# Gated linear attention on one core: TensorE's order written down, with small fp32 products in fewer runs

## The chip, the cores and the metric

One Trainium2 chip, one of its cores. The metric is device time in microseconds, from the first to the last instruction of one execution and what lies around it; lower is better. The kernel before took 1204.29 us (median of 3 runs, 1204.18 to 1205.54).

The engines by the names of the profile: PE is TensorE (matmul; PEld its weight loads), DVE is VectorE, ACT is ScalarE, POOL is GpSimd, SP is SyncE, which issues most DMAs. Each engine works through its own list of instructions in order; semaphores tie the lists together.

## The reference, cut to what matters

The program is two layers of a decoder trunk for 512 tokens of width 1024. Layer 1 has chunked gated linear attention (GLA) as its mixer, with 4 heads, keys of 128 and values of 256 per head. The change lies in this mixer alone.

```python
q, k, v, g_lr, og = _split(h @ w_in, GLA_SPLITS)
log_a = jax.nn.log_sigmoid(g_lr @ w_gate_up + gate_bias) / GLA_GATE_NORMALIZER
...
def step(state, inp):                       # one chunk of tokens
    qi, ki, vi, gi = inp                    # gi: cumulative sum of log_a in the chunk
    g_end = gi[:, :, -1, :]
    o_inter = einsum('bhtd,bhdv->bhtv', qi * exp(gi), state)
    decay = exp(where(causal, gi[t] - gi[s], -inf))
    scores = einsum('bhtd,bhsd,bhtsd->bhts', qi, ki, decay)
    o_intra = einsum('bhts,bhsv->bhtv', scores, vi)
    state = exp(g_end) * state + einsum('bhsd,bhsv->bhdv', ki * exp(g_end - gi), vi)
    return state, o_inter + o_intra
...
o = _rms_norm(o, o_norm) * silu(og)
return o @ w_out
```

## The kernel before

**Two kinds of matmul.** The large products (`mm3`, lines 162 to 164) split both operands into a rounded high part and the rest, and add high x high, high x low and low x high: three matmuls of 512, 368 or 336 columns. They make the queries, keys and output gates (`feature`: 24 matmuls each, into a `ps` bank of PSUM) and the values (`Values.step`: 48 matmuls for half of the depth, into all four `ps` banks). Their weights are loaded by SP, rounded by ScalarE (`wh`, line 142) and subtracted by VectorE (`wl`, line 143), three buffers each.

The small products work on plain fp32 and write `pa` banks of PSUM, of which there are four too. A head needs, in this order:

- `base`: VectorE's cumulative sum `G` of the log decays, and the product for the diagonal; `diag` (line 1762): a product with ones that gives the scores' diagonal
- `decay` and `level` (lines 1797 and 1800): the scores are built by levels of blocks of 64, 32, 16, 8 (`lo`) and 4 (`hi`). VectorE and ScalarE make a tile `F` of keys and queries times decays for each level, TensorE multiplies it with itself in tiles of 128x64, one `pa` bank per level, and VectorE copies what the mask keeps into the scores (lines 1808, 1810)
- `decay_pairs` and `level_pairs` (line 1835): the blocks of 2 and 1 together, also in 128x64 tiles; four masked copies (lines 1841, 1846)
- `decay_off` and `off` (line 1879): three transposes of the decayed keys; ScalarE copies them out (`kt`, line 1881)
- `state` (line 1893): the chunk states, six matmul records into two banks; ScalarE and VectorE carry them on (lines 1901, 1896)
- `read` (lines 1917, 1919): scores x values plus queries x states, into two banks; ScalarE squares (line 1923), a root is taken on GpSimd, VectorE scales (line 1927)
- `turn` (line 1934): eight transposes of the head's output into two banks; ScalarE scales them into `oT` (line 1938)

`log_decays` transposes the low-rank gate (line 1711), multiplies it by the gate's up-projection (line 1722) and takes the log sigmoid. `gate` makes an output gate (silu on ScalarE, line 1677), `gated` multiplies it with a turned output. `load_vectors_ffn(1)` turns two vectors of the next block's convolution (line 222), whose DMAs landed near the start of the program. The tiles `F`, `E`, `Es`, `Ec` and `kt` share one pool of eight buffers (`new`).

**What sets the order.** The stage's calls stand at the end of `mixer1`. No engine's order is written down there: a planner orders each engine by the place in the program and by its own estimate of when operands and buffers are ready. In the profile TensorE's order follows the calls, with some groups held back and single large products put between: `diag(0)` stands ahead of `query(w, 2)`; three large products stand between `level(2, lo)` and `read(0)`, and one inside `read(0)`; four stand between `turn(0)` and `state(1)`, three between `level(3, lo)` and `read(1)`, and two, four and four stand around `level(3, hi)` and `off(3)`. Elsewhere in the program, in other stages, TensorE's order is written by hand with `tc.manual_schedule(engines={ET.PE})`: inside this block the instructions of the named engines keep the order of the calls, and the planner still orders the others.

Of the kernel before, what the change touches and what calls it, by code (L numbers as in the profile page):

```python
# [14 lines left out]
ALU = mybir.AluOpType  # L15
# [7 lines left out]
ND = D // P  # L23
# [4 lines left out]
GH, GDK, GDV, GR = 4, 128, 256, 16  # L28
ET = mybir.EngineType
# [27 lines left out]
class Kernel:  # L57
# [1557 lines left out]
    def mixer1(self):  # L1615
# [4 lines left out]
        with tc.tile_pool(name="m1", bufs=1) as mp:  # L1620
# [5 lines left out]
            class Values:  # L1626
# [5 lines left out]
                        self.weights(w_in[:, k0 : k0 + 4, 1024 + c0 : 1024 + c1], 4, v.n, by="a") for k0 in (0, 4)  # L1632
                    ]

                def step(v, i):
                    c0, n, vn = v.c0, v.n, v.vn
                    if i == 0:
                        v.pss = [self.ps() for _ in range(NT)]
                    for k in range(4 * i, 4 * i + 4):
                        for t in range(NT):  # L1640
                            self.mm3(
                                v.pss[t][:, :n], tok(k, t), v.ws[i](k % 4, 0, n), start=k == 0, stop=k == ND - 1
                            )
                    for t in range(NT if i else 0):
                        rt = r[:, t : t + 1]
                        if n > vn:
                            nc.scalar.activation(glr[:, t, :], v.pss[t][:, vn:n], AF.Copy, scale=rt)
                        nc.scalar.activation(vt[t][:, c0 : c0 + vn], v.pss[t][:, :vn], AF.Copy, scale=rt)
# [3 lines left out]
            def pair_w(c0):  # L1652
                return self.weights(w_in[:, :, c0 : c0 + 256], ND, 256)

            def feature(w, c):
                ps = self.ps()
                for k in range(ND):
                    self.mm3(ps, w(k, c * P, (c + 1) * P), xg[k], start=k == 0, stop=k == ND - 1)
                return ps

            def query(w, h):
                o = qT[h] = self.fp.tile([P, S], F32, tag="a0", name=self.nm("qT"))
                nc.vector.scalar_tensor_tensor(
                    out=o, in0=feature(w, h % 2), scalar=float(GDK**-0.5), in1=R, op0=ALU.mult, op1=ALU.mult
                )

            def key(w, h):
                o = kT[h] = self.fp.tile([P, S], F32, tag="a0", name=self.nm("kT"))
                ps = feature(w, h % 2)
                with tc.high_priority(offset=60):  # L1670
                    nc.vector.tensor_tensor(o, ps, R, ALU.mult)
# [32 lines left out]
                nc.vector.tensor_tensor(ws[64:96], w[64:96], t[64:96].bitcast(F32), ALU.subtract)  # L1704
                return ws

            def log_decays():

                ps = self.pa()
                for t in range(NT):  # L1710
                    nc.tensor.transpose(ps[:GR, t * P : (t + 1) * P], glr[:, t, :], self.ident)
                gT = self.sp.tile([P, S], F32R, tag="R", name="gT")
                nc.vector.tensor_copy(
                    gT[:96].rearrange("p (a b) -> p a b", b=P), self.ones[:96].unsqueeze(1).to_broadcast([96, NT, P])
                )
                nc.scalar.activation(gT[:GR], ps[:GR], AF.Copy)
                nc.scalar.activation(gT[64 : 64 + GR], ps[:GR], AF.Copy)
                nc.vector.tensor_tensor(gT[32 : 32 + GR], ps[:GR], gT[:GR].bitcast(F32), ALU.subtract)
                es, pzs = [], []
                for h in range(GH):  # L1720
                    pz = self.pa()
                    mm(pz, wgs[:96, h * GDK : (h + 1) * GDK], gT[:96], start=True, stop=True)
                    e = new()
                    nc.scalar.activation(e, pz, AF.Abs)
                    pzs.append(pz)
                    es.append(e)
                for e in es:
                    nc.scalar.activation(e, e, AF.Exp, scale=-1.0)
                for e in es:
                    nc.scalar.activation(e, e, AF.Ln, bias=1.0)  # L1730
                for h, (e, pz) in enumerate(zip(es, pzs)):
                    la = mp.tile([P, S], F32, tag=f"lah{h}", name=self.nm("la"))
                    nc.vector.scalar_tensor_tensor(
                        out=la, in0=pz, scalar=0.0, in1=e, op0=ALU.min, op1=ALU.subtract
                    )
                    las.append(la)
# [10 lines left out]
            def base(h):  # L1747

                G = Gs[h] = mp.tile([P, S], F32, tag="G", name=self.nm("G"), bufs=2)
                nc.vector.tensor_tensor_scan(  # L1750
                    G, run.rearrange("p a b -> p (a b)"), las[h], 0.0, op0=ALU.mult, op1=ALU.add
                )
                sc = scores[h] = mp.tile([P, GDV * NT], F32, tag="sc", name=self.nm("sc"), bufs=3)

                pr = Fs[h, "diag"] = new()[:, : S // 2]
                nc.vector.tensor_tensor(pr, ev(kT[h]), ev(qT[h]), ALU.mult)
                nc.gpsimd.memset(sc[:, :S], 0.0)

            def diag(h):
                sc = scores[h]  # L1760
                pd = self.pa()[:, : S // 2]
                mm(pd, self.ones, Fs[h, "diag"], start=True, stop=True)
                nc.vector.tensor_tensor(
                    sc[:, :S].rearrange("p (a n b) -> p a n b", a=NT, b=2)[:, :, :, 0],
                    pd.rearrange("p (a n) -> p a n", a=NT),
                    ev(self.ident).unsqueeze(1).to_broadcast([P, NT, P // 2]), ALU.mult,
                )
# [106 lines left out]
            def off(h):  # L1874

                Es, Ec, tot = Fs[h, "off"]
                pt = self.pa()
                for i in range(NT - 1):
                    nc.tensor.transpose(pt[:, i * P : (i + 1) * P], Es[:, i * P : (i + 1) * P], self.ident)
                kt = new()  # L1880
                nc.scalar.copy(kt[:, : 3 * P], pt[:, : 3 * P])
                Fs[h, "kt"] = kt
# [70 lines left out]
            v.step(1)  # L1953
            R = self.spread()
            w = pair_w(0)
            query(w, 0)
            log_decays()
            query(w, 1)
            w = pair_w(512)
            key(w, 0)  # L1960
            key(w, 1)
            w = pair_w(256)
            base(0)
            diag(0)
            decay(0, lo)
            query(w, 2)
            level(0, lo)
            decay(0, hi)
            decay_off(0)
            decay_pairs(0)  # L1970
            query(w, 3)
            w = pair_w(768)
            level(0, hi)
            off(0)
            base(1)
            decay(1, lo)
            key(w, 2)
            level_pairs(0)
            diag(1)
            key(w, 3)  # L1980
            v = Values(0, 336, 336)
            level(1, lo)
            decay(1, hi)
            decay_off(1)
            decay_pairs(1)
            v.step(0)
            level(1, hi)
            off(1)
            base(2)
            decay(2, lo)  # L1990
            v.step(1)
            v = Values(336, 672, 336)
            level_pairs(1)
            diag(2)
            state(0)
            decay(2, hi)
            decay_off(2)
            v.step(0)
            level(2, lo)
            read(0)  # L2000
            decay_pairs(2)
            level(2, hi)
            off(2)
            base(3)
            decay(3, lo)
            v.step(1)
            w = pair_w(2064)
            level_pairs(2)
            diag(3)
            turn(0)  # L2010
            state(1)
            decay(3, hi)
            decay_off(3)
            gate(w, 0)
            level(3, lo)
            read(1)
            decay_pairs(3)
            state(2)
            gate(w, 1)
            turn(1)  # L2020
            w = pair_w(2064 + 256)
            self.load_vectors_ffn(1)
            level(3, hi)
            off(3)
            read(2)
            level_pairs(3)
            gate(w, 2)
            turn(2)
            state(3)
            gated(0)  # L2030
            gated(1)
            gate(w, 3)
            w = pair_w(2064 + 512)
            read(3)
            gated(2)
            gated(3)
            gate(w, 4)
            turn(3)
            gated(4)
            gate(w, 5)  # L2040
            w = pair_w(2064 + 768)
            gated(5)
            for m in (6, 7):
                gate(w, m)
                gated(m)
        return lambda done, then: self.project(self.rows(a["gla_w_out"][0]), ys, done, then)

    def run(self):
# [34 lines left out]
```

## Time and profile before

| | |
|---|---|
| median of 3 runs | 1204.29 us (1204.18 to 1205.54) |
| the profiled execution | 1203.8 us, span 1202.0 us |
| TensorE busy | 1194.0 us, 99% of the span |
| VectorE busy | 989.3 us, 82% |
| ScalarE busy | 681.1 us, 57% |
| GpSimd busy | 43.7 us, 4% |
| chain that ended last | TensorE 89%, VectorE 6%, ScalarE 2% |
| the stage that the change orders | 602.2 to 739.3 us |

How to read the rows: a row of the timeline has the start in us, the duration, the engine, the line, the operation, what it writes and reads, the shapes, and how many neighbours of the same kind it stands for; idle time of the engine before it and what ended that stands in brackets. `128*64` is the part of TensorE's array that a product uses. Matmuls are pipelined, so a record lasts past the start of the next one; what one costs is the distance from start to start. Full fp32 products of 256 columns appear as two records each. A row of a stretch has, after the stretch and its length, the busy time and number of instructions of PE, PEld, DVE, ACT and POOL, the granted clock, the DMA share and GB/s. A row of waits has who waited, for whom, the total, how often and the longest.

### The profile page before, as it was taken

Reading aid. Unit: us, or ns where it says so; the run is one execution under the profiler, and the core shown is the slowest. Engines: PE = TensorE matmul, PEld = TensorE weight load, DVE = VectorE, ACT = ScalarE, POOL = GpSimd, SP = SyncE. Lnnn points to the kernel's source line nnn. Section 1 sums busy time; section 2 is a strip of 40 time slices with the busy share of each in tenths; the row PEclk is TensorE's granted clock in tenths of the full one; section 3 lists DMA queues with packets and bytes.
Section 4 is the critical chain, followed back from the end, with each engine's and each line's share of the span. In section 5 each row is a group of like instructions: output and inputs, shape, how many; then the busy total and the mean of one; then the engine's idle time right before and its main releaser. Section 6 shows DMA issues by size and latency. Waiting matters only on the chain.

```text
span 1202.0 us, 17888 instructions
## 1 busy us (share of the span) xinstructions
PE 1194.0 (99%) x7085; PEld 1037.6 (86%) x7085; DVE 989.3 (82%) x1563; ACT 681.1 (57%) x1109; POOL 43.7 (4%) x64
## 2 busy tenths in 40 slices
PE   9999999999999999999999999999999999999998
PEld 8877788999899889888988988889999999888887
DVE  6786587899999996789769876677999999978595
ACT  7466465656555744566563555565555656645374
POOL 2600000000000000000100000000000000000000
PEclk9999999999999999999999999999999999999999
DMA  7221322323233342232422222313242423322501
GB/s 222 90 88 39 97 79 70 129 83 119 92 104 107 107 139 97 97 106 63 140 66 69 71 71 70 106 54 122 71 140 71 139 72 128 127 88 97 210 1 70
DMA packets 110839, 117.61 MB, mean 98 GB/s; under 512 B 2808, under 2 KB 105778, under 8 KB 110756
## 3 DMA queue, kind: packets, MB, share of 16 engines
q1 hardware_dynamic: 109920, 115.88, 29.7%
q8 instruction: 55, 0.90, 0.3%
q0 software_dynamic: 560, 0.42, 0.3%
q10 hardware_dynamic: 276, 0.18, 0.1%
q14 instruction: 28, 0.23, 0.1%
HBM read 114.37 MB, written 2.10 MB: 97 GB/s over the span
## 4 chain that ended last, share of the span: by engine, by line
PE 89%; DVE 6%; ACT 2%; issue 1%; POOL 1%; DMA 0%; SPq 0%; DVEq 0%; ACTq 0%; POOLq 0%
PE ps L162 11%; PE ps L163 11%; PE ps L164 11%; PE pa L163 7%; PE pa L162 7%; PE pa L164 7%; PE ps L879 6%; PE ps L881 6%; PE ps L880 6%; PE pa L879 2%; PE pa L881 2%; PE pa L880 2%; DVE wl L143 1%; PE ps L1484 1%; PE ps L1483 1%
## 5 line engine op out<-in xcount | busy, mean ns | idle before, releaser
L142 ACT ACTIVATE wh<-raw 128x1024 fp32r<-128x1024 f32 (+4 forms) x146 | 145.8, 999 | 124.5 <-PE ps L163 78.8
L143 DVE TENSOR_TENSOR wl<-raw,wh 128x1024 fp32r<-128x1024 f32 (+4 forms) x146 | 168.1, 1151 | 40.7 <-ACT wh L142 39.9
L826 ACT ACTIVATE wh<-raw 128x1024 fp32r<-128x1024 f32 x84 | 89.2, 1062 | 120.6 <-DVE raw L851 65.1
L939 DVE SCALAR_TENSOR_TENSOR zt<-z,vfa,zt 128x510 f32<-128x510 f32 (+1 forms) x176 | 130.6, 744 | 5.3 <-ACT zt L937 4.7
L827 DVE TENSOR_TENSOR wl<-raw,wh 128x1024 fp32r<-128x1024 f32 x84 | 102.6, 1221 | 21.3 <-ACT wh L826 21.2
L937 ACT ACTIVATE zt<-z,vfb 128x512 f32<-128x512 f32 x88 | 71.0, 810 | 21.5 <-DVE four L990 8.3
L162 PE MATMUL ps<-b,wh 128*128 128x512 f32 x192 | 76.8, 400 | 0.0
L163 PE MATMUL ps<-b,wh 128*128 128x512 f32 x192 | 75.1, 391 | 0.0
L164 PE MATMUL ps<-b,wl 128*128 128x512 f32 x192 | 75.0, 391 | 0.0
L879 PE MATMUL ps<-four,wh 128*128 128x256 f32 x248 | 69.4, 280 | 0.7 <-ACT ps L904 0.7
L163 PE MATMUL pa<-a,wh 128*128 128x512 f32 x176 | 69.0, 392 | 0.0
L163 PE MATMUL pa<-b,wh 128*128 128x512 f32 x176 | 69.0, 392 | 0.0
L162 PE MATMUL pa<-a,wh 128*128 128x512 f32 x176 | 69.0, 392 | 0.0
L162 PE MATMUL pa<-b,wh 128*128 128x512 f32 x176 | 69.0, 392 | 0.0
L881 PE MATMUL ps<-four,wl 128*128 128x256 f32 x248 | 68.8, 277 | 0.0
L880 PE MATMUL ps<-four,wh 128*128 128x256 f32 x248 | 68.6, 277 | 0.0
L164 PE MATMUL pa<-a,wl 128*128 128x512 f32 x176 | 68.4, 389 | 0.0
L164 PE MATMUL pa<-b,wl 128*128 128x512 f32 x176 | 68.4, 389 | 0.0
L162 PE MATMUL ps<-a,wh 128*128 128x512 f32 x128 | 50.6, 395 | 0.0
L162 PE MATMUL ps<-uh,wh 128*128 128x512 f32 x128 | 50.3, 393 | 0.0
L163 PE MATMUL ps<-a,wh 128*128 128x512 f32 x128 | 50.2, 392 | 0.0
L163 PE MATMUL ps<-ul,wh 128*128 128x512 f32 x128 | 50.1, 391 | 0.0
(488 smaller groups left out, 3577.4 us busy)
## 6 DMA issues: line engine op xcount, KB each, us to landing
raw<-in_ffn_w_up_dram SPq DMA_DIRECT2D x44, 1024.0 KB, 5.0
raw<-in_ffn_w_down_dram SPq DMA_DIRECT2D x13, 1024.0 KB, 4.8
raw<-in_hy_w_in_dram SPq DMA_DIRECT2D x8, 1024.0 KB, 5.1
raw<-in_gla_w_in_dram SPq DMA_DIRECT2D x8, 1024.0 KB, 5.2
raw<-in_ffn_w_down_dram SPq DMA_DIRECT2D x8, 768.0 KB, 4.2
raw<-in_ple_w_gate_dram SPq DMA_DIRECT2D x6, 1024.0 KB, 4.8
raw<-in_hy_w_out_dram SPq DMA_DIRECT2D x16, 256.0 KB, 4.0
raw<-in_gla_w_out_dram SPq DMA_DIRECT2D x4, 1024.0 KB, 4.8
```

The lines of the kernel that those rows point to most:

```text
L142: nc.scalar.activation(hv, v, AF.Copy)
L143: nc.vector.tensor_tensor(lv, v, hv.bitcast(F32), ALU.subtract)
L162: mm(out, lh, rh, start=start, stop=False, **kw)
L163: mm(out, lh, rl, start=False, stop=False, **kw)
L164: mm(out, ll, rh, start=False, stop=stop, **kw)
L826: nc.scalar.activation(h, src, AF.Copy)
L827: nc.vector.tensor_tensor(l, src, h.bitcast(F32), ALU.subtract)
L879: mm(out, wh, xh, start=first and j == 0, stop=False, **kw)
L880: mm(out, wh, xl, start=False, stop=False, **kw)
L881: mm(out, wl, xh, start=False, stop=j == ND // 2 - 1, **kw)
L937: nc.scalar.activation(y, z, AF.Identity, scale=w2[:, f : f + 1], bias=bb[:, f : f + 1])
L939: nc.vector.scalar_tensor_tensor(out=y[:, tap:], in0=z[:, : S - tap], scalar=w[:, f : f + 1], in1=y[:, tap:], op0=ALU.mult, op1=ALU.add,)
```

## The change

The calls from `query(w, 0)` to the last `gated(m)` stand inside `tc.manual_schedule(engines={ET.PE})`, so TensorE follows them as written. The calls are reordered: `diag(0)` goes behind `query(w, 2)`, next to `level(0, lo)`; `base` and `decay(h, lo)` of the next head go ahead of `level(h, hi)`, `off(h)`, `level_pairs(h)` and the next `diag`, which stand together; `read(0)`, `level(2, hi)` and `off(2)` stand between the halves of a `v.step(1)`; `load_vectors_ffn(1)` stands ahead of `turn(1)`, and `level_pairs(3)` ahead of `read(2)`. `log_decays` is divided: the transposes and the rounding of the gate (`turned_gates`) come behind `query(w, 0)`, the products in the middle of `query(w, 1)`. For this `feature`, `query` and `step` take a function `mid` that they call halfway.

```diff
-                def step(v, i):
+                def step(v, i, mid=None):
...
                     for k in range(4 * i, 4 * i + 4):
+                        if mid and k % 4 == 2:
+                            mid()
...
-            def feature(w, c):
+            def feature(w, c, mid=None):
                 ps = self.ps()
                 for k in range(ND):
+                    if mid and k == ND // 2:
+                        mid()
...
-            def log_decays():
+            def turned_gates():
...
+                return gT
+
+            def log_decays(gT):
...
+            with tc.manual_schedule(engines={ET.PE}):
+                query(w, 0)
+                gT = turned_gates()
+                query(w, 1, lambda: log_decays(gT))
+                w = pair_w(512)
+                key(w, 0)
+                key(w, 1)
+                w = pair_w(256)
+                base(0)
+                decay(0, lo)
+                query(w, 2)
+                diag(0)
+                level(0, lo)
+                decay(0, hi)
+                decay_off(0)
+                decay_pairs(0)
+                query(w, 3)
+                w = pair_w(768)
+                base(1)
+                decay(1, lo)
+                key(w, 2)
+                level(0, hi)
+                off(0)
+                level_pairs(0)
+                diag(1)
+                key(w, 3)
+                v = Values(0, 336, 336)
+                level(1, lo)
+                decay(1, hi)
+                decay_off(1)
+                decay_pairs(1)
+                v.step(0)
+                base(2)
+                decay(2, lo)
+                v.step(1)
+                v = Values(336, 672, 336)
+                level(1, hi)
+                off(1)
+                level_pairs(1)
+                diag(2)
+                state(0)
+                decay(2, hi)
+                decay_off(2)
+                v.step(0)
+                level(2, lo)
+                decay_pairs(2)
+                base(3)
+                decay(3, lo)
+
+                def reading():
+                    read(0)
+                    level(2, hi)
+                    off(2)
+
+                v.step(1, reading)
+                w = pair_w(2064)
+                level_pairs(2)
+                diag(3)
+                turn(0)
+                state(1)
+                decay(3, hi)
+                decay_off(3)
+                gate(w, 0)
+                level(3, lo)
+                read(1)
+                decay_pairs(3)
+                state(2)
+                gate(w, 1)
+                w = pair_w(2064 + 256)
+                self.load_vectors_ffn(1)
+                turn(1)
+                level(3, hi)
+                off(3)
+                level_pairs(3)
+                read(2)
+                gate(w, 2)
+                turn(2)
+                state(3)
...
+                read(3)
...
+                turn(3)
```

The rest of the calls, shown as `...` at the end, keep their order.

More of the change, by code (lines that the diff above doesn't have):

```diff
@@ L1653, in pair_w, with query @@
                 return self.weights(w_in[:, :, c0 : c0 + 256], ND, 256)
-            def feature(w, c):
+            def feature(w, c, mid=None):
                 ps = self.ps()
                 for k in range(ND):
+                    if mid and k == ND // 2:
+                        mid()
                     self.mm3(ps, w(k, c * P, (c + 1) * P), xg[k], start=k == 0, stop=k == ND - 1)
                 return ps
-            def query(w, h):
+            def query(w, h, mid=None):
                 o = qT[h] = self.fp.tile([P, S], F32, tag="a0", name=self.nm("qT"))
                 nc.vector.scalar_tensor_tensor(
-                    out=o, in0=feature(w, h % 2), scalar=float(GDK**-0.5), in1=R, op0=ALU.mult, op1=ALU.mult
+                    out=o, in0=feature(w, h % 2, mid), scalar=float(GDK**-0.5), in1=R, op0=ALU.mult, op1=ALU.mult
                 )
@@ L1955, in mixer1 @@
             w = pair_w(0)
[L1956 to L2045, printed above, removed]
+            with tc.manual_schedule(engines={ET.PE}):
[74 more added lines that the diff above has]
+                state(3)
+                gated(0)
+                gated(1)
+                gate(w, 3)
+                w = pair_w(2064 + 512)
+                read(3)
+                gated(2)
+                gated(3)
+                gate(w, 4)
+                turn(3)
+                gated(4)
+                gate(w, 5)
+                w = pair_w(2064 + 768)
+                gated(5)
+                for m in (6, 7):
+                    gate(w, m)
+                    gated(m)
```

## The prediction

> **What bounds the kernel now.** I read the page first (busy time, the slices, the chain that ended last), then the busy time of each engine by stretches of the GLA stage, then TensorE's timeline there, and beside each suspicious place VectorE's or ScalarE's timeline. The profiled execution took 1203.8 us, 1202.0 of span and 1.8 around it; the median of the runs is 1204.29, so 0.5 above it.
>
> ```profile
> span 1202.0 us, 17888 instructions
> PE 1194.0 (99%) x7085; PEld 1037.6 (86%) x7085; DVE 989.3 (82%) x1563; ACT 681.1 (57%) x1109; POOL 43.7 (4%) x64
> ```
>
> TensorE is busy 99%: no stage can gain by overlap, only by cheaper transitions or by the few waits that are left. The stage that the change orders runs from the four gate transposes, just behind query 0, to the last turn:
>
> ```profile
> 602.19 0.60 PE L1711 MATMUL pa<-cf,glr 128*16 128x128 f32 x4
> 738.29 1.04 PE L1934 MATMUL pa<-cf,sc 128*128 128x128 f32 x8
> 626.00:646.00 20.00, 20.00 (x163) 16.22 (x162) 19.73 (x51) 8.54 (x17) 0.00 (x0) 1.00 0.12 35
> ```
>
> In the last row, of the stretch 626 to 646, the first engine is TensorE, the third VectorE: busy 20.00 and 19.73 of 20 us, at a granted clock of 1.00. VectorE is as full as TensorE. What TensorE reaches earlier there, it waits for.
>
> **The change, part by part.** Between the two rows above, TensorE now leaves its large products 23 times for small fp32 ones (counted in its timeline). Written down, it leaves them 14 times. What is one such visit worth? Two kinds:
>
> ```profile
> 675.32 0.31 PE L163 MATMUL ps<-wl,b 128*128 128x336 f32 x1
> 675.47 0.32 PE L164 MATMUL ps<-wh,b 128*128 128x336 f32 x1
> 675.72 0.62 PE L1800 MATMUL pa<-F 128*64 128x64 f32 x7
> 676.20 1.57 PE L1797 MATMUL pa<-F 128*64 128x32 f32 x47
> 677.70 0.42 PE L162 MATMUL ps<-wh,b 128*128 128x336 f32 x1
> 677.96 0.32 PE L163 MATMUL ps<-wl,b 128*128 128x336 f32 x1
> ```
>
> Starts count, since matmuls overlap. A product of 336 columns follows the one before after 0.15 us (675.32 to 675.47). The last one before the narrow `128*64` products takes 0.25, the first one behind them 0.26: 0.21 lost at these edges, and about 0.3 with the slower first and last narrow product inside the merged rows. The other kind is full width, `128*128`:
>
> ```profile
> 713.60 0.39 PE L164 MATMUL ps<-b,wl 128*128 128x512 f32 x1
> 713.84 0.49 PE L1879 MATMUL pa<-cf,F 128*128 128x128 f32 x3
> 714.08 0.48 PE L162 MATMUL ps<-b,wh 128*128 128x512 f32 x1
> 714.39 0.40 PE L163 MATMUL ps<-b,wh 128*128 128x512 f32 x1
> ```
>
> From 713.60 to 714.39 are 0.79 us, for two large products (0.23 each) and three transposes (0.11 each): 0.01 over. So leaving the large products for full-width fp32 ones is nearly free; what costs is the change to 64 columns and back. Each head has three such groups (the low levels, the high level, the pairs): twelve before. In the written order every joined pair of them still has `off`'s transposes between, full width, so it is twelve after. Term 1: nine visits fewer at 0.01, **-0.1 us**; bounds 0 and -0.9 (three heads have their high level and pairs joined, 0.3 each, if a return across transposes were free).
>
> The Trainium skill (TensorEngine Tiling, Tiling Modes, Key Properties) says that a change of the tiling mode drains TensorE, while another tile of the same mode does not. That speaks against the change: the joins that save a visit don't save a change of mode. By the opposite reading, that any exchange of large for small products drains, nine visits at 0.3 would give -2.7 instead of -0.1; the trace, with 0.01 and 0.3, goes by the rule.
>
> Term 2, waits that go. The diagonal of head 0 stood alone and too early, and the gate products followed 11 large ones where 12 stand now:
>
> ```profile
> 604.91 0.39 PE L163 MATMUL ps<-b,wh 128*128 128x512 f32 x1
> 605.24 1.20 PE L1722 MATMUL pa<-gT,wgs 96*128 96x512 f32 x4
> 619.89 0.39 PE L164 MATMUL ps<-b,wl 128*128 128x512 f32 x1
> 620.31 0.70 PE L1762 MATMUL pa<-F,ones_r 128*128 128x256 f32 x2
> ```
>
> The product before takes 0.33 and 0.42 in place of 0.23, and the first one behind a wait is slower (the four gate products hold TensorE for 1.04, their 1.20 less the 0.16 by which the last overlaps the next, in place of 0.92): 0.1 more each. That is 0.2 and 0.3, together 0.5 us. But the order also puts `level(0, hi)` and `off(0)` (634.06 to 634.95, 0.89 us) behind `key(w, 2)`, so key 2 is reached 0.89 + 0.5 earlier, at 633.6, and its weights are not there:
>
> ```profile
> 634.06 0.66 PE L1797 MATMUL pa<-F 128*64 128x32 f32 x16
> 634.95 0.47 PE L162 MATMUL ps<-b,wh 128*128 128x512 f32 x1
> 632.87 1.22 DVE L143 TENSOR_TENSOR wl<-raw,wh 128x1024 fp32r<-128x1024 f32 x1
> ```
>
> The low half of key 2's weights is ready at 634.1 by VectorE, which has a full queue from the decay chains and does the same work before it in either order. TensorE waits there for 0.5 us and the gain is gone: **0 us**; bounds -0.5 (VectorE cuts the weights sooner) and +0.2. The second wait in this stretch, for key 3's bank, stays as it is, because `v.step(0)` still follows `level(1, lo)`:
>
> ```profile
> 650.64 0.32 PE L164 MATMUL ps<-wh,b 128*128 128x336 f32 x1
> 651.18 0.43 PE L162 MATMUL ps<-wh,b 128*128 128x336 f32 x1 [0.23 <-DVE kT L1671]
> ```
>
> That is 0.54 for 0.15: 0.4 us that VectorE's order may remove or double; **0**, bounds -0.5 and +0.8.
>
> Term 3, waits that come. All small products write the four `pa` banks. Where a run needs more than four, its later products wait until VectorE or ScalarE has emptied the first. The planner put single large products into these places; the written order takes them out. Four places:
>
> (a) Head 1's high level, transposes, pairs, head 2's diagonal and `state(0)` need six banks. How long are the groups between, and how soon does VectorE empty a high level's bank?
>
> ```profile
> 689.36 0.69 PE L1835 MATMUL pa<-qT,kT 128*64 128x64 f32 x16
> 689.98 0.70 PE L1762 MATMUL pa<-F,ones_r 128*128 128x256 f32 x2
> 636.53 0.59 DVE L1808 COPY_PREDICATED sc<-msk,pa 64x128 f32<-64x128 uint8 x2
> 712.92 0.61 DVE L1808 COPY_PREDICATED sc<-msk,pa 64x128 f32<-64x128 uint8 x2
> ```
>
> Pairs take 0.62, the diagonal some 0.5 (its 0.70 less the overlap), transposes 0.24 to 0.3: `state(0)` comes about 1.5 us behind the high level. The bank was empty at 637.1 for products that ended at 634.7 (2.4 us), and at 713.5 for products that ended at 712.9 (0.6; this group's row is under d). The wait is 0.9 or none: **+0.4 us**, bounds 0 and +0.9.
>
> (b) Pairs of head 2, diagonal 3, `turn(0)`, `state(1)`: six banks again. Before, four large products stood ahead of `state(1)`, and it still started only as ScalarE had emptied `turn(0)`'s bank:
>
> ```profile
> 692.37 1.80 PE L1893 MATMUL pa<-vt,F 128*128 128x256 f32 x6
> 690.69 1.05 ACT L142 ACTIVATE wh<-raw 128x1024 fp32r<-128x1024 f32 x1
> 691.63 0.68 ACT L1938 ACTIVATE oT<-pa,vec 128x512 f32<-128x512 f32 x1
> ```
>
> 692.3 is ScalarE's time, behind a weight cut of 1.05 us that it took first. The four large products (0.23 each) move behind and leave a hole of **+0.9 us**; bounds +0.1 (the turn goes ahead of the cut) and +1.8 (the second half waits as long).
>
> (c) `read(1)` directly behind `level(3, lo)`, which holds all four banks; three large products stood between:
>
> ```profile
> 700.63 0.50 PE L162 MATMUL ps<-b,wh 128*128 128x512 f32 x1
> 701.43 0.60 PE L1917 MATMUL pa<-vt,sc 128*128 128x256 f32 x2
> 700.47 0.41 DVE L1810 COPY sc<-pa 64x256 f32<-64x256 f32 x1
> ```
>
> The first bank is free at 700.9, TensorE would come at 700.6: 0.3 and a slower first product, **+0.4 us**; bounds 0 and +0.8 (the whole gap).
>
> (d) The longest run: two vector transposes, `turn(1)`, high level, transposes and pairs of head 3, `read(2)`: nine banks from four. Ten large products (2 + 4 + 4) filled it:
>
> ```profile
> 711.54 0.48 PE L162 MATMUL ps<-b,wh 128*128 128x512 f32 x1
> 712.21 0.66 PE L1797 MATMUL pa<-F 128*64 128x32 f32 x16
> 715.10 1.02 PE L1917 MATMUL pa<-vt,sc 128*128 128x256 f32 x4
> 711.50 0.66 ACT L1938 ACTIVATE oT<-pa,vec 128x512 f32<-128x512 f32 x1
> 714.01 0.67 ACT L1938 ACTIVATE oT<-pa,vec 128x512 f32<-128x512 f32 x1
> ```
>
> The high level started at 712.21, as ScalarE had finished the first `oT` (711.50 + 0.66), and the second `oT` came only behind a silu, at 714.7. With ScalarE's work in that order, all ten (2.3 us) turn into holes. But the vector transposes now come first and have small copies, and pairs ahead of `read(2)` give ScalarE 0.6 more, so a good part may be covered: **+1.1 us**, about the middle; bounds +0.2 and +2.3. The vector transposes' own DMAs landed long before and add no wait; nothing moves on the queues of SP and POOL, whose issues keep their places around it.
>
> `read(0)` moves from 3 large products behind `level(2, lo)` to 24, so 3.2 us later (21 at 0.15); `turn(0)` still follows it by the high level, 24 large products, pairs and a diagonal, some 5 us, which its squares, root and scalings have: **0**, bounds 0 and +0.5.
>
> Sum: -0.1 + 0 + 0 + 0.4 + 0.9 + 0.4 + 1.1 = +2.7, which makes 1206.5 for an execution like the profiled one and **1206.9** against the median. Behind the stage nothing is edited.
>
> **The rivals.** First, covered: the planner knows the written order and gives its evictions other places, so (a) and (c) cost nothing and (b) and (d) their low ends, 0.1 + 0.2, less 0.1: 1204.5. For it: ScalarE is busy 57% only. Against it: the bank times above are ScalarE's and VectorE's, at two places, (b) and (d), within 0.1 us of TensorE's start.
>
> Second, not slower: the joins pay after all. The array's return across a few transposes costs nothing (three joins, 0.9), and no wait comes while all old ones go (0.5 in term 2, 0.4 for key 3, 0.4 in the late `state(1)`): 1204.3 - 2.2 = 1202.1. It decides if `off`'s transposes inside a run begin and end without the 0.1 us edges. Against it: full width and 64 columns meet there exactly as at the edges that the rows show.
>
> Third, the `F` buffers. Eight exist; `base(2)` and `decay(2, lo)` now stand ahead of `level(1, hi)` and `off(1)`, and ten would be live (`Ec` and `kt` of head 0, three of head 1, one diagonal, four levels). Such a wait exists already:
>
> ```profile
> DVE F L1859 <- PE pa L1800: 1.7, 1, 1.7
> ```
>
> If two levels of head 2, and so for head 3, start that much later each costs 1.2 on top, the 1.7 of this row less about 0.5 that (a) counts already: 1206.9 + 2.4 = 1209.3. Against it: VectorE idled 1.7 us in that very wait.
>
> **How the numbers follow.** Chances: the forecast 0.50, covered 0.33, joins pay 0.07, buffers 0.10. About 0.2% (2.4 us) is what a measurement of this kernel can tell from no change; 1206.7 is that line, so of the forecast's 0.50 0.38 lie above it and 0.12 below. Slower: 0.38 + 0.10 = 0.48, and 0.02 of covered: 0.50. Faster by over 0.2% needs 1201.9: 0.04 of the joins and 0.02 of covered, 0.06. The rest is 0.44. Range: the low ends of (a) to (d) with a gain of 1 us give 1203.6, the rival of the buffers 1209.3 and a little: 1203.4 to 1209.5. The likeliest one's own range is 1205.5 to 1208.5.
>
> **What would show it.** TensorE's timeline of the changed kernel would show 14 visits; edges of 0.1 us still at twelve narrow groups; `state(1)` directly behind `turn(0)` with a hole of 0.5 to 1 us that ends with `oT`; holes ahead of the high level or the pairs of head 3 that end with ScalarE; key 2 waiting for `wl`. The prediction is wrong if the runs pass without holes, or if idle time appears where VectorE's decay factors are waited for.

## The result, and the profile after

The changed kernel took 1210.95 us (median of 6 runs, 1209.86 to 1212.02) against 1204.52 of the kernel before beside it (6 runs, 1203.98 to 1205.74): a ratio of 1.0053, 95% interval 1.0043 to 1.0063. It is 6.4 us slower; the prediction's sum was 2.7, and its range ended at 1209.5.

The profiled execution took 1211.58 us, 7.78 more than the one of before. First its page (the span; TensorE's busy time):

```profile
span 1209.8 us, 17890 instructions
PE 1196.2 (99%) x7085; PEld 1039.7 (86%) x7085; DVE 990.4 (82%) x1563; ACT 682.5 (56%) x1109; POOL 43.6 (4%) x64
```

TensorE still shows 99%: the tenths of a page hide 6 us in 1200. Its timeline at the two ends of the stage shows where they lie:

```profile
602.59 0.60 PE L1715 MATMUL pa<-cf,glr 128*16 128x128 f32 x4
...
746.05 1.03 PE L1942 MATMUL pa<-cf,sc 128*128 128x128 f32 x8
```

From the gate transposes to the last turn are 143.46 us, where they were 136.10: 7.36 of the 7.78 lie in the stage. (Another 0.4 lie in query 0 ahead of it, behind a late copy; the kernel with ten buffers, below, has them too.) The same timeline in the joined runs:

```profile
626.77 1.10 PE L1805 MATMUL pa<-F 128*64 128x32 f32 x31
629.07 0.62 PE L1805 MATMUL pa<-F 128*64 128x32 f32 x15 [1.20 <-DVE sc L1771]
...
667.16 0.70 PE L1770 MATMUL pa<-F,ones_r 128*128 128x256 f32 x2
668.43 1.13 PE L1901 MATMUL pa<-vt,F 128*128 128x256 f32 x4 [0.57 <-ACT F L1889]
670.41 0.70 PE L1901 MATMUL pa<-vt,F 128*128 128x256 f32 x2 [0.85 <-DVE sc L1816]
...
691.81 0.32 PE L164 MATMUL ps<-wh,b 128*128 128x336 f32 x1
693.89 0.69 PE L1843 MATMUL pa<-qT,kT 128*64 128x64 f32 x16 [1.76 <-DVE sc L1935]
695.25 0.90 PE L1770 MATMUL pa<-F,ones_r 128*128 128x256 f32 x2 [0.67 <-DVE sc L1935]
695.94 1.92 PE L1942 MATMUL pa<-cf,sc 128*128 128x128 f32 x8
697.78 2.16 PE L1901 MATMUL pa<-vt,F 128*128 128x256 f32 x6
699.59 0.58 PE L162 MATMUL ps<-b,wh 128*128 128x512 f32 x1
...
718.50 0.66 PE L1805 MATMUL pa<-F 128*64 128x32 f32 x16
720.26 0.52 PE L1887 MATMUL pa<-cf,F 128*128 128x128 f32 x3 [1.10 <-DVE sc L1816]
```

Four places have idle time. Below, a hole is the distance from start to start less what the same step takes where it doesn't wait, here or in a kernel below (691.81 to 693.89 is 2.08, and ahead of narrow products the last large one takes 0.25: 1.83).

| place | hole, us | what ended it |
|---|---|---|
| head 0's low levels | 1.39 | the diagonal's bank, VectorE (L1771) |
| both halves of `state(0)` | 0.67 + 1.14 = 1.81 | ScalarE's copy `kt` (L1889), then the high level's bank |
| ahead of `level_pairs(2)` and of `diag(3)` | 1.83 + 0.74 = 2.57 | `read(0)`'s scalings, VectorE (L1935) |
| head 3's high level to `off(3)` | 1.17 | the high level's bank, VectorE (L1816) |

The eight transposes of `turn(0)` then last 1.92 where the eight of the last turn last 1.03, without a wait. The granted clock explains it. In this profile it changes only at multiples of 3.41 us, counted from where its record begins (6.12 us into the span). By stretches of that length, the column behind POOL's is the clock:

```profile
692.20:695.61 3.41, 1.05 (x18) 0.87 (x18) 2.68 (x8) 1.93 (x4) 0.63 (x1) 1.00 0.00 0
695.61:699.03 3.42, 3.42 (x13) 2.65 (x12) 2.69 (x6) 1.85 (x3) 0.52 (x1) 0.50 0.00 0
699.03:702.44 3.41, 3.41 (x16) 2.85 (x16) 2.20 (x7) 1.00 (x2) 0.00 (x0) 1.00 0.02 5
```

Behind the holes TensorE ran at half its clock for one such stretch. From `diag(3)` to the end of `state(1)` (695.25 to 699.59) are 4.34 us; the same products at full clock take 2.63 (a kernel below: 3.13 with a wait of 0.50 in it), so this costs some 1.7.

Together the holes are 6.94, with the clock 8.6. Against it waits of before are gone: key 3's bank 0.4, the diagonal's 0.3, the gate products' 0.2, and smaller ones.

### The profile page after: what moved, and what is told of

It reads as the page before. It is cut to its first block, busy times and chain, and to the rows that moved or that the text cites. A ratio compares the mean times of both kernels' runs of the same rounds, so it can differ in the third digit from the quotient of the medians.

```text
span 1209.8 us, 17890 instructions
## 1 busy us (share of the span) xinstructions
PE 1196.2 (99%) x7085; PEld 1039.7 (86%) x7085; DVE 990.4 (82%) x1563; ACT 682.5 (56%) x1109; POOL 43.6 (4%) x64
## 4 chain that ended last, share of the span: by engine, by line
PE 89%; DVE 6%; ACT 3%; issue 1%; POOL 1%; DMA 1%; DVEq 0%; ACTq 0%; POOLq 0%
PE ps L162 12%; PE ps L163 12%; PE ps L164 12%; PE pa L163 7%; PE pa L162 7%; PE pa L164 7%; PE ps L879 6%; PE ps L881 6%; PE ps L880 6%; PE pa L879 2%; PE pa L881 2%; PE pa L880 2%; DVE wl L143 1%; PE ps L1484 1%; PE ps L1482 1%
## 5 line engine op out<-in xcount | busy, mean ns | idle before, releaser
L143 DVE TENSOR_TENSOR wl<-raw,wh 128x1024 fp32r<-128x1024 f32 (+4 forms) x146 | 168.1, 1152 | 39.4 <-ACT wh L142 38.3
L164 PE MATMUL ps<-b,wl 128*128 128x512 f32 x192 | 74.8, 390 | 0.0
L164 PE MATMUL pa<-b,wl 128*128 128x512 f32 x176 | 68.4, 389 | 0.0
L164 PE MATMUL pa<-a,wl 128*128 128x512 f32 x176 | 68.4, 389 | 0.0
```

The costliest lines, as they stand in the source:

```text
L143: nc.vector.tensor_tensor(lv, v, hv.bitcast(F32), ALU.subtract)
L164: mm(out, ll, rh, start=False, stop=stop, **kw)
```

## The experiments

Theory A, from the trace after: the written order as such loses what the planner's single large products did for the bank waits. Rival B: a second cause lies in the moved calls, `base` and `decay` of the next head ahead of the high level, which fill the eight `F` buffers. Rival C: the diagonal moved to the low levels. Two more questions are whether a joined run saves anything once no hole is in it, and what the clock costs.

**The calls of before, unmoved, written down**

```diff
+            with tc.manual_schedule(engines={ET.PE}):
-            query(w, 0)
-            log_decays()
+                query(w, 0)
+                log_decays()
...
```

> The calls of the kernel before, unchanged, inside the block that writes TensorE's order down: no call is moved, only the planner's single large products between the groups go (3 and 1 at read 0, 4 ahead of state 1, 3 ahead of read 1, 2, 4 and 4 in head 3's run, 11 in front of the gate products). Theory A (the holes come from writing the order down, since nothing fills the waits for the four pa banks): +2 to +4 us against the kernel before, holes ahead of state 1, read 1, the high level and the transposes of head 3. Theory B (the moved calls are the cause: the joined runs and the later read 0): within 1 us of the kernel before.

Measured: 1211.55 us (1209.8 to 1213.12), ratio 1.006 [1.0045, 1.0075]. That is 7.2 slower without one call moved. Its timeline and its stretches:

```profile
602.47 0.60 PE L1711 MATMUL pa<-cf,glr 128*16 128x128 f32 x4
605.51 1.60 PE L1722 MATMUL pa<-gT,wgs 96*128 96x512 f32 x4 [2.44 <-DVE gT L1718]
606.90 0.63 PE L162 MATMUL ps<-b,wh 128*128 128x512 f32 x1
607.33 0.63 PE L163 MATMUL ps<-b,wh 128*128 128x512 f32 x1
```

```profile
602.68:606.09 3.41, 0.97 (x7) 0.58 (x5) 2.58 (x3) 1.92 (x4) 0.00 (x0) 1.00 0.06 7
606.09:609.50 3.41, 3.41 (x10) 2.67 (x9) 0.00 (x0) 3.38 (x6) 0.00 (x0) 0.50 0.91 299
```

With nothing between the gate's transposes and its products, TensorE waits 2.44 us for VectorE's copies, and in the stretch at half clock behind it large products take 0.43 (606.90 to 607.33) instead of 0.23. The other holes are 1.4 ahead of `state(1)`, 0.6 ahead of head 3's high level, 0.9 behind it and 0.7 ahead of `read(2)`: the places (b) and (d) of the prediction.

**The moved calls, with TensorE's order left to the planner**

```diff
-            with tc.manual_schedule(engines={ET.PE}):
-                query(w, 0)
+            query(w, 0)
...
```

> The moved calls of the changed kernel, but the planner orders TensorE again: by its list it puts 13 large products inside state 0, 5 into pairs, diagonal and turn, 6 behind the high level of head 3, 4 ahead of read 1. Theory A (missing fillers): most of the 6.4 us comes back, about 1206 to 1207; the hole in the low levels of head 0 stays (1.4 us), since the order there is the same. Theory B (the moved calls themselves): the time stays within 1.5 us of the changed kernel, 1209.5 or more.

Measured: 1205.27 us (1204.59 to 1205.69), ratio 1.0008 [0.9999, 1.0018]. The planner put single large products back into most of the runs, and 5.7 of the 6.4 us are gone (5.5 when each kernel is taken against the runs of before beside it). What it left:

```profile
628.08 0.66 PE L1805 MATMUL pa<-F 128*64 128x32 f32 x16 [1.20 <-DVE sc L1771]
...
691.07 0.69 PE L1843 MATMUL pa<-qT,kT 128*64 128x64 f32 x16 [0.54 <-DVE sc L1935]
```

So filled runs hide the cause B too; this run alone doesn't say how much of the loss is B's.

**The diagonal of head 0 ahead of query 2 again**

```diff
+                diag(0)
                 query(w, 2)
-                diag(0)
                 level(0, lo)
```

> The changed kernel with one move undone: the diagonal of head 0 stands ahead of query 2 again, so the run of diagonal and low levels needs four banks instead of five. If the fifth bank is what the last low level waits for, its hole of 1.4 us goes, the old wait of the diagonal (0.3) comes back, and the time falls by about 1 us. Rival: VectorE bounds this stretch; the hole then moves to key 2, which waits for its weights, and the time stays.

Measured: 1209.92 us (1209.73 to 1211.7), ratio 1.0052 [1.0035, 1.0069]. The hole of 1.39 is gone; the diagonal's old wait (0.39) and a wait of key 2 for its weights (0.36) come instead. By this trace 0.6 us is C's; the medians are 1.0 apart, but the runs of the two kernels overlap. The other holes stand unchanged, yet in this execution the clock stayed (its stretches of 3.41 us lie elsewhere here):

```profile
693.29 0.69 PE L1843 MATMUL pa<-qT,kT 128*64 128x64 f32 x16 [1.76 <-DVE sc L1935]
694.65 0.70 PE L1770 MATMUL pa<-F,ones_r 128*128 128x256 f32 x2 [0.67 <-DVE sc L1935]
```

```profile
689.55:692.97 3.42, 1.98 (x13) 1.70 (x12) 2.59 (x9) 3.02 (x7) 1.01 (x1) 1.00 0.51 180
692.97:696.38 3.41, 2.28 (x26) 1.79 (x26) 3.35 (x9) 1.56 (x3) 0.00 (x0) 1.00 0.00 0
```

**Ten `F` buffers instead of eight** in the changed kernel

```diff
-            new = lambda: mp.tile([P, S], F32, tag="F", name=self.nm("F"), bufs=8)
+            new = lambda: mp.tile([P, S], F32, tag="F", name=self.nm("F"), bufs=10)
...
-                ws, t = (mp.tile([P, S], F32R, tag="F", name=self.nm("wgs"), bufs=8) for _ in range(2))
+                ws, t = (mp.tile([P, S], F32R, tag="F", name=self.nm("wgs"), bufs=10) for _ in range(2))
```

> The changed kernel with ten F buffers for eight, nothing else. If the kt copy of off(1) and off(2) starts late because its buffer is taken by the decay factors that are now made earlier, the copy comes right behind the transposes: the first hole of state 0 (0.7 us) goes and the second hole of the run of head 2's pairs (0.9 us) shrinks, together -1 to -2 us. If the buffers don't matter, the time stays within 0.5 us and the holes stay where they are.

Measured: 1206.19 us (1205.62 to 1206.63), ratio 1.0015 [1.0006, 1.0024]: 4.8 less (4.5 when each is taken against the runs of before beside it), and TensorE's order is the same instruction for instruction; VectorE's, which the planner makes, is not. Its timeline:

```profile
667.37 0.70 PE L1770 MATMUL pa<-F,ones_r 128*128 128x256 f32 x2
667.97 1.53 PE L1901 MATMUL pa<-vt,F 128*128 128x256 f32 x6
...
691.06 0.70 PE L1770 MATMUL pa<-F,ones_r 128*128 128x256 f32 x2
691.60 1.04 PE L1942 MATMUL pa<-cf,sc 128*128 128x128 f32 x8
692.98 1.56 PE L1901 MATMUL pa<-vt,F 128*128 128x256 f32 x6 [0.34 <-ACT oT L1946]
694.19 0.59 PE L162 MATMUL ps<-b,wh 128*128 128x512 f32 x1
```

The holes in `state(0)` and at the pairs are gone, and with them the half clock; (b), `state(1)` behind `turn(0)`, shows for the first time (0.50). The low levels (1.37) and `off(3)` (1.17) stay. How the buffers did it shows in the changed kernel's waits (who waits for whom: total, times, longest) and timelines of ScalarE and VectorE:

```profile
DVE F L1867 <- PE pa L1808: 2.6, 1, 2.6
ACT F L1889 <- PE pa L1770: 2.3, 2, 2.0
...
DVE F L1784 <- PE pa L1805: 1.8, 1, 1.8
```

```profile
667.90 0.48 ACT L1889 COPY F<-pa 128x384 f32<-128x384 f32 x1 [0.23 <-PE pa L1770]
```

```profile
687.77 0.42 DVE L1784 TENSOR_TENSOR F<-G 128x256 f32<-128x256 f32 x1
...
691.25 0.41 DVE L1786 TENSOR_TENSOR F<-G 128x256 f32<-128x256 f32 x1
691.59 0.16 DVE L171 TENSOR_SCALAR rs<-ss 128x4 f32<-128x4 f32 x1
...
692.86 0.88 DVE L1935 TENSOR_SCALAR sc<-pa,rq 128x256 f32<-128x256 f32 x2 [0.80 <-POOL rq L172]
```

`kt` needs a tile of the pool and gets one only as `diag(2)`, the product just ahead of `state(0)`, has read its own: the run waits for itself. VectorE's decays wait for tiles in the same way and come late; those of head 3 stand as a block of 3.8 us (687.77 to 691.59) ahead of the root's input for `read(0)` (L171). In the kernel with ten tiles that instruction runs at 687.20.

**Eight buffers, but `base` and the low decays of heads 2 and 3 behind `off` again**; TensorE's order is unchanged

```diff
                 v.step(0)
-                base(2)
-                decay(2, lo)
                 v.step(1)
...
                 off(1)
+                base(2)
+                decay(2, lo)
...
-                base(3)
-                decay(3, lo)
...
                     off(2)
+                    base(3)
+                    decay(3, lo)
```

> The changed kernel with eight F buffers and exactly its TensorE order; only the calls that make heads 2 and 3's running sums and low decay factors (base and decay) stand behind off(1) and off(2) again, as before, so that VectorE's and ScalarE's order changes and the factors no longer take the buffers ahead of the kt copies. If the early factors in eight buffers are the cause, the holes in state 0 (0.7 and 1.0 us) and ahead of head 2's pairs (1.9 and 0.9) go without any more buffers: 1206 to 1207. If the holes come from too few PSUM banks in the joined runs or from read 0's late place, they stay, since TensorE's order is the same: 1209.5 or more.

Measured: 1207.72 us (1206.66 to 1208.04), ratio 1.0026 [1.0016, 1.0037], 3.2 less than the change. Most of the wait in `state(0)` (0.2 is left ahead of the diagonal there) and the holes at the pairs go again, by a second way. In their place `state(1)` waits for the turn, its whole price now bare (a hole of 1.99):

```profile
691.33 1.04 PE L1942 MATMUL pa<-cf,sc 128*128 128x128 f32 x8
694.19 1.56 PE L1901 MATMUL pa<-vt,F 128*128 128x256 f32 x6 [1.82 <-ACT oT L1946]
```

**Ten buffers in the kernel before**

> The kernel before with ten F buffers and nothing else: the control for the run with ten buffers. If the buffers were short only in the new order, it stays within 1 us of the kernel before (1204.3). If ten buffers simply make this stage faster, it falls by as much as the changed kernel did with them, 4 to 5 us.

The edit is that of the run above. Measured: 1203.92 us (1203.49 to 1204.5), ratio 0.9997 [0.9988, 1.0006]. The old calls don't lack tiles; the moved ones do.

**All holes filled**: ten buffers, the diagonal in the middle of query 2, three large products ahead of `state(1)`, six between head 3's high level and `off(3)`, `read(2)` ahead of the pairs

```diff
-                query(w, 2)
-                diag(0)
+                query(w, 2, {4: lambda: diag(0)})
...
-                state(1)
-                decay(3, hi)
-                decay_off(3)
-                gate(w, 0)
+                gate(w, 0, {1: lambda: (state(1), decay(3, hi), decay_off(3))})
...
-                off(3)
-                level_pairs(3)
-                read(2)
-                gate(w, 2)
+                gate(w, 2, {2: lambda: (off(3), read(2), level_pairs(3))})
```

> The changed kernel with ten F buffers and three of its joins opened again by hand: head 0's diagonal in the middle of query 2, three large products between turn 0 and state 1, six between head 3's high level and its transposes, with read 2 ahead of the pairs. With ten buffers holes of 1.4, 0.5 and 1.3 us are left at just these places. If they are waits for banks, all three go, with 0.3 given back at key 2's weights: about 1203.3, 1 us below the kernel before. If VectorE or ScalarE bound these places, the holes move behind the fillers and the time stays above 1205.

Measured: 1204.03 us (1203.32 to 1205.46), ratio 0.9997 [0.9988, 1.0006]. A written order without those holes is as fast as the planner's, with fewer visits, and no faster: the joins save nothing that can be measured. One wait is left, the one that the prediction put at key 2:

```profile
633.89 0.39 PE L163 MATMUL ps<-b,wh 128*128 128x512 f32 x1
634.98 0.50 PE L164 MATMUL ps<-b,wl 128*128 128x512 f32 x1 [0.70 <-DVE wl L143]
```

**Ten buffers, moved calls, planner's order**

> The moved calls with ten F buffers, TensorE's order left to the planner, which now lists one filler of 2 products ahead of state 1 and one of 6 behind head 3's high level. The hole in head 0's low levels (1.4) stays, the one ahead of head 2's pairs (0.7 with eight buffers) goes: about 1204.5. If it is slower than the handwritten order with ten buffers (1206.2), the planner's own VectorE order is at fault.

This combines two edits shown above. Measured: 1204.44 us (1203.48 to 1205.26), ratio 1.0001 [0.9992, 1.0009]. The diagonal's hole of 1.40 stands in it, and the whole is still level with before.

**The calls of before written down, with the gate products in the middle of query 1**

```diff
                 query(w, 0)
-                log_decays()
-                query(w, 1)
+                gT = turned_gates()
+                query(w, 1, lambda: log_decays(gT))
```

> The order before written down call by call took 1211.55 us, with one hole of 2.61 us ahead of the gate products (VectorE empties the transposes' banks behind a feature that was issued earlier) and TensorE's clock at a half for some 4 us behind it. Here the transposes stand ahead of query 1 and the products in its middle, as in the changed kernel; nothing else of that order is moved. If the hole and the low clock behind it (six to nine large products 0.2 us slower each, 1.2 to 1.8 us) both go: 1207 to 1207.8. If the low clock has another cause and stays: about 1209. If the hole only moves to the next wait: 1211 to 1212.

Measured: 1207.93 us (1207.03 to 1209.38), ratio 1.0032 [1.0022, 1.0041]: 3.6 less than without the split. Of ten executions five took 1207.0 to 1207.6 and four 1209.2 to 1209.4. In the profiled one, of 1207.31 us, the hole of 2.6 is gone:

```profile
605.72 1.07 PE L1727 MATMUL pa<-gT,wgs 96*128 96x512 f32 x4
```

1209.8, the fastest execution without the split and the only one of its four with a clock of 1.000, less 2.6 is 1207.2. In the profiled execution without the split, of 1210.96 us, the half clock cost some 1.5 more (six large products at 0.43, the gate products at 1.39 in place of 1.04); the two slower ones weren't profiled.

**The filled kernel, with head 0's high level and `off` ahead of key 2**

```diff
+                level(0, hi)
+                off(0)
                 key(w, 2)
-                level(0, hi)
-                off(0)
                 level_pairs(0)
```

> As the kernel with ten F buffers and large products in three of the small runs (1204.03 us), with the high level and the transposes of head 0 ahead of key 2 again, where the kernel before has them. There TensorE waited 0.86 us for key 2's low weights. If that wait is what is left of the stage's loss, 0.9 us go and the hole at key 2 is under 0.1: 1203.1. If VectorE sets the pace there, the wait comes back a little later (key 3, or the values' first step) and the time stays at 1204.0. One more visit to the large products is 0.01 by the trace and can't be seen; if a visit cost 0.3, it would be 1203.4.

Measured: 1204.15 us (1203.57 to 1204.81), ratio 0.9998 [0.999, 1.0007]. Key 2's wait is gone, and about as much, 1.0, comes back 30 us later, in front of `state(0)`:

```profile
665.45 0.70 PE L1770 MATMUL pa<-F,ones_r 128*128 128x256 f32 x2
667.07 1.53 PE L1901 MATMUL pa<-vt,F 128*128 128x256 f32 x6 [0.92 <-DVE sc L1816]
```

VectorE is as full as TensorE between the two places (busy 30.55 of the 31.00 us from 636 to 667), which fits that it sets the pace there: the place where TensorE waits could be chosen here, the wait not. No order tried beats the kernel before by more than a measurement can tell.

## Why the prediction was wrong

**Term 1 was right.** TensorE leaves its large products 14 times, and the visit that joins head 0's high level, transposes, pairs and head 1's diagonal keeps the edges of its parts:

```profile
640.76 0.66 PE L1805 MATMUL pa<-F 128*64 128x32 f32 x16
641.35 0.55 PE L1887 MATMUL pa<-cf,F 128*128 128x128 f32 x3
641.83 0.69 PE L1843 MATMUL pa<-qT,kT 128*64 128x64 f32 x16
642.44 0.70 PE L1770 MATMUL pa<-F,ones_r 128*128 128x256 f32 x2
642.79 0.58 PE L162 MATMUL ps<-b,wh 128*128 128x512 f32 x1
```

Over what its products take without edges this visit has 0.63 us; its two halves had 0.28 and 0.35 as visits of their own. The rival of paying joins falls.

**Term 2 saw the gain and not the price.** It counted the diagonal's move to the low levels as a wait that goes. But a diagonal and four low levels need five banks of four, and nothing large stands between: 1.39 us, of which the run with the diagonal put back returned 0.6 by its trace. That is the rule with which Term 3 began, not applied to this fifth place. Key 2's wait for its low weights, 0.5 in the text, was 0.36 and 0.86 where no earlier hole hid it. The 0.5 itself was misread: only the third product of a group (L164) reads them, 0.46 behind the first, so the rows gave less than 0.1. The rest came because VectorE cut them later, from 633.7 instead of 632.9.

**Term 3, (a)**: 0.4 forecast, 1.81 measured, and for another reason in its first half: `kt` had no tile. With ten tiles it was 0. **(b)**: 0.9 forecast. The mechanism is the one named, a turn's bank behind ScalarE, at 0.50, 1.99 and 1.4 in three kernels; in the changed kernel the holes ahead of it gave ScalarE the time. **(c)**: 0.4 forecast, 0.2 measured, a slower first product without a bank wait. **(d)**: 1.1 forecast, 1.17 measured, but at `off(3)` and behind VectorE, which had begun a weight cut of 1.22 us (L143) ahead of the copy; the prediction had looked for ScalarE there, so the size is luck. (The sum of the terms makes 1207.0 against the median, not 1206.9.)

**The step that failed is the price and chance of the `F` buffers, with `read(0)` at 0.** The rival counted ten live tiles, and ten buffers were enough; but it priced them at 2.4 us and gave them 0.10, because VectorE had idled in such a wait before. They cost 4.8 (3.2 by the other way of undoing them, which lays (b) bare). VectorE's idle time was not the measure: the late decays pushed `read(0)`'s scalings behind them, and these hold the banks that the pairs of head 2 need. The step on `read(0)` asked whether the turn would have its input, and not who needs the bank that its scalings empty. So the prediction's own sign of being wrong, idle time behind the decay factors, came at one remove: TensorE waited for scalings that stood behind them. Of the 6.4 us these 4.8 are the buffers', the clock behind their holes included; the 1.6 to 1.9 left are the holes of 1.37, 0.50 and 1.17, less the waits of before that went. The two causes don't add up: the planner's fillers alone, with eight buffers, took away 5.7, since large products stand where TensorE would have waited.

## What to carry to other kernels

When an order is written down, count for each run of small products the banks it fills against those there are, and put a large product wherever the count passes; this holds for every join, not only for the long ones. Count the tiles of the pools in the same way, since moving the making of operands ahead of their use lengthens lives, and a run can then wait for a tile that it holds itself. Where another engine is as full as TensorE, a wait removed at one place can come back at the next, as key 2's did here; then a shorter order is worth what it takes off that engine. Holes close together can also halve the clock, so filling them can give back more than their length (with ten buffers the holes went and the 1.7 us of half clock with them).

## What the runs showed of the hardware

Idle time costs more than itself when the clock follows it, and it did so at holes I hadn't thought long enough. Idle times of 1.76 and 0.67 us close behind each other were followed by 3.41 us at half clock in the profile of the changed kernel, which cost some 1.7, and not in that of the kernel with the diagonal back, with the same two idle times; 2.44 us were, and 1.82 us were not.

The traces show what decides. In all twelve profiles the clock changes only at multiples of 3.41 us from where its record begins, 4.3 to 7.5 us into the span. Every stretch of this grid in which TensorE was idle for 2.01 us or more was followed by half clock: 2.36 and 2.44 in the two kernels above, and at the end of the program 2.01, 2.15 and 2.82 in three profiles, or, in the others, a stretch that was idle throughout. No stretch with 1.82 us or less was. In the kernel with the diagonal back the two idle times fall into two stretches, with 1.44 and 1.14. So it is the idle share of a stretch that counts, not the length of one idle time, and where a hole falls on the grid is luck. The line lies between these two stretches, of the kernel with the late decays (TensorE busy 1.59 us, so idle 1.82; clock 1.00 in the next stretch) and at the end of the calls of before written down (busy 1.41, idle 2.01; 0.50 in the next):

```profile
692.06:695.47 3.41, 1.59 (x10) 1.22 (x8) 3.40 (x12) 2.72 (x6) 0.52 (x1) 1.00 0.00 0
1203.42:1206.84 3.42, 1.41 (x12) 1.20 (x11) 1.69 (x4) 0.95 (x2) 0.00 (x0) 1.00 0.18 64
```

The kernel with the split gates leaves a question open. Its five executions of 1207.0 to 1207.6 had mean clocks of 0.999 to 1.000, the four of 1209.2 to 1209.4 had 0.998 to 0.999, 2 us apart with nothing edited. In its profiled execution, one of the five, no 3.41 us in the stage hold more than 1.8 us of idle time, wherever the grid lies; the four weren't profiled, and such a mean also counts the idle end of the program. So it isn't shown that a stretch at half clock made the difference.

The Trainium skill (TensorE: Matmul & The Clock Gate, Part 1) says that the clock is halved after an idle window of about 3.4 us, and that the window runs freely, so that it depends on the phase. The window's length and the dependence on the phase agree with what is seen here. That the whole window must be idle doesn't: 2.01 us of it were enough, and no single idle time in the stage reached 2.5 us.
